# A hybrid trunk on one core: 50 units of the second layer's MLP weights get their lower parts beside the first MLP, and the first layer's MLPs end by halves of tokens

## The chip, the cores and the metric

The kernel runs on one core of a Trainium2 chip. The time is the device time of one execution in microseconds (us). The median of the runs counts; one further execution was profiled. The core has five engines that each work through a list of their own in order: TensorE (PE) multiplies matrices into PSUM, VectorE (DVE), ScalarE (ACT) and GpSimd (POOL) work element by element, and SyncE (SP) issues most of the DMAs. An instruction that waits holds up everything behind it in its engine's list.

## The reference

A decoder trunk of two layers for 1024 tokens of width 1024. Layer 0 mixes the tokens with a state-space model (S5), layer 1 with an attention in which an indexer picks 256 keys for each query. A squared-ReLU MLP of width 4096 follows each mixer. Every sub-layer has a norm before and one after it. All is in float32.

```python
def sq_relu_mlp(h, w1, w2):
    a = jax.nn.relu(h @ w1)
    return (a * a) @ w2

def reference(...):
    h = x
    for i in range(DEPTH):
        pre = rms_norm(h, norm_g[i, 0])
        mix = s5_mixer(pre, ...) if i % 2 == 0 else dsa_mixer(pre, ...)
        h = h + rms_norm(mix, norm_g[i, 1])
        ff = sq_relu_mlp(rms_norm(h, norm_g[i, 2]), mlp_w1[i], mlp_w2[i])
        h = h + rms_norm(ff, norm_g[i, 3])
    return h
```

## The kernel before

**Precision.** A product of float32 matrices is made of three matmuls of a shorter type. Each operand is split into an upper part (a rounded copy) and a lower part (what the rounding left). `mm3` (lines 156 to 161) then adds upper by upper, upper by lower and lower by upper.

**A weight unit.** The weights come in units of 128 x 1024 numbers, 512 KB. `unit` (line 119) loads one into a buffer `wr` (three of them) from SP's queue (line 127). In two halves of 512 columns ACT makes the upper part (line 142) and a subtraction the lower part (line 143), on DVE for the first half and on POOL for the second. Both land in a buffer `wh` of 2 x 512 numbers (six of them, so three units). A unit feeds 24 matmuls of 512 columns.

**The halves of the sequence.** All of the work is done for 512 tokens at a time; the first 512 tokens are half 0, the others half 1. A block is 128 x 2 x 512 numbers: 256 of the 1024 features for 512 tokens, and four blocks are one activation.

**An MLP.** `mlp` (line 281) does one layer's MLP for one half. It has 32 units of w1 and 32 of w2. `pair` (line 297) computes two units of w1, applies ReLU (line 306), squares (line 308) and splits. For each of eight chunks `c` four units of w2 add to four accumulators `acc` in SBUF (line 341). A generator `side` may be handed over. After every unit `beside` (line 289) draws steps from it, `per` of them, after `wait` units without any; these steps are written down with a priority of 500 over the MLP's own. With `finish` (line 316), which the last MLP of the kernel uses, the last four units are loaded into buffers of their own (`wl`, eight). Then the last chunk is done for 256 tokens and again for the other 256 (`th`), and `finish` is called after each with its part of the accumulators.

**The norms.** `post_norm` (line 221) takes an MLP's or a mixer's result, sums its squares (`squares`, line 179: squares on ACT, sums of blocks at line 193, then small matmuls with ones at line 196), takes the inverse root (`rsqrt`, line 163), spreads it over the partitions by PE transposes (line 238) and a copy (line 240), multiplies (line 252) and adds the residual (line 262), which comes back from DRAM (`hd`). `pre_norm` (line 199) multiplies by the gain and splits into upper and lower parts (lines 208 and 209), then sums squares again. `att_r` (line 1165) turns the inverse root into tables for the rotary embedding, with PE transposes (line 1179) of what ACT copies (line 1177).

**The order of the work.** In `run` (line 1242): S5 for both halves; the MLP of layer 0, half 0, without side work (line 1257), called the first MLP here; its norms (line 1258); the MLP of layer 0, half 1 (line 1267), the second MLP, and beside it half 0's projections and attention; its norms (line 1269); half 0's attention output and the index projections of half 1 (lines 1271 to 1275); the residual of half 0 (line 1287); the MLP of layer 1, half 0 (line 1289), the third MLP, and beside it half 1's projections, top-k and attention; at last the MLP of layer 1, half 1 (line 1298), the fourth, with `finish`.

**Who sets each engine's order.** The kernel writes the operations down in program order. A planner then simulates them with modelled costs, takes at each moment the ready operation of the highest priority, fixes every engine's list and every buffer's address from that, and adds the semaphores. The chip keeps to those lists even where its times differ from the modelled ones. The names of the buffers in the profile are those of the pools' tags and tiles; MLP activations appear as `b`, PSUM for the MLP as `m`, for norms as `c`, for the rest as `p`.

Of the kernel before, what the change touches and what calls it, by code (L numbers as in the profile page):

```python
# [7 lines left out]
F32 = mybir.dt.float32  # L8
F32R = mybir.dt.float32r
# [3 lines left out]
ALU = mybir.AluOpType  # L13
AX = mybir.AxisListType

BUFS = {"par": 1, "bc": 2, "tb": 1, "sb": 1, "bb": 2,
        "s5": 14, "cs": 2, "sq5": 8, "cst": 2, "u": 1,
        "x": 8, "xa": 8, "acc": 4, "hid": 9, "b": 22, "ld": 3, "q": 2}
EPS = 1e-6
# [7 lines left out]
STEPS_BEST = 2  # L27

WAIT_OUT = 1

PRIORITY = 500

# [22 lines left out]
class Trunk:  # L55
# [60 lines left out]
        t = t.rearrange("p (a b) -> p a b", a=shape[1]) if len(shape) > 2 else t  # L116
        return t if dt == F32 else t.bitcast(dt)

    def unit(self, src, last=False, heads=False, raw=None):

        nc = self.nc
        self.n += 1
        if raw is None:
            raw = self.wp.tile([128, 1024], F32, name=f"wr{self.n}", tag="wr", bufs=3)
        nc.sync.dma_start(raw, src)
        out = []
        for h in range(2):
            t = self.wp.tile([128, 2, 512], F32R, name=f"wh{self.n}_{h}", tag="wl" if last else "wh",  # L130
                             bufs=8 if last else 6)
            hi, lo = t[:, 0], t[:, 1]
            r = raw[:, h * 512:(h + 1) * 512]
            out.append((hi, lo))
            if heads:
                rs = r.rearrange("p (k h e d) -> p e k h d", h=2, e=2, d=32)
                his, los = [q.rearrange("p (k e h d) -> p e k h d", h=2, e=2, d=32) for q in (hi, lo)]
                parts = [(his[:, e], los[:, e], rs[:, e]) for e in range(2)]
            else:
                parts = [(hi, lo, r)]  # L140
            for ph, pl, pr in parts:
                nc.scalar.activation(ph, pr, AF.Copy)  # L142
                (nc.gpsimd if h else nc.vector).tensor_sub(pl, pr, ph.bitcast(F32))  # L143
        return out
# [51 lines left out]
            nc.tensor.matmul(ps[:, j:j + 1], acc[:, j * 128:(j + 1) * 128], self.ones, start=True, stop=True)  # L196
        return ps[:, :n // 128]

    def pre_norm(self, h, gi, tag="b", square=True):


        nc = self.nc
        out = []
        for j, b in enumerate(h):
            hi, lo = [self.blk([128, 2, 512], F32R, tag=tag) for _ in range(2)]
            for q in range(2):
                g = self.gain[:, gi, 2 * j + q:2 * j + q + 1]
                nc.scalar.activation(hi[:, q], b[:, q], AF.Copy, scale=g)
                nc.vector.scalar_tensor_tensor(lo[:, q], b[:, q], g, hi.bitcast(F32)[:, q],  # L209
                                               op0=ALU.mult, op1=ALU.subtract)  # L210
            out.append((hi, lo))
        s = self.squares(h, nc.gpsimd.tensor_add if square else nc.vector.tensor_add)
        r = self.small([128, 4], F32, "kept")
        nc.vector.tensor_scalar(r, s, 1.0 / 1024, EPS, op0=ALU.mult, op1=ALU.add)
        if square:
            nc.vector.scalar_tensor_tensor(r, r, 1024 * EPS, r, op0=ALU.mult, op1=ALU.mult)
        else:
            nc.vector.tensor_copy(r, self.rsqrt(r, 4)[:, :4])
        return out, r

    def post_norm(self, f, gi, h, e=None, reorder=False, last=None, aside=False):
# [56 lines left out]
            self.nc.sync.dma_start(dst[j], h[j])  # L278


    def mlp(self, L, x, side=None, per=0, wait=0, finish=None):


        nc = self.nc
# [4 lines left out]
        def beside():  # L289
            due[0] += self.per  # L290
            self.units += 1
            while side and due[0] >= 1:
                due[0] -= 1
                with self.tc.high_priority(offset=PRIORITY):
                    next(side, None)

        def pair(p):
            r = self.blk([128, 2, 512], tag="hid")
            for j in range(2):
                w = self.unit(w1[L, 2 * p + j])  # L300
                ps = self.pm()
                for kt in range(8):
                    o = (kt % 4) * 128
                    self.mm3(ps, [t[:, o:o + 128] for t in w[kt // 4]],
                             [t[:, kt % 2] for t in x[kt // 2]], kt == 0, kt == 7)
                nc.scalar.activation(r[:, j], ps, AF.Relu)  # L306
                if j:
                    nc.scalar.activation(r, r, AF.Square)  # L308
                    hid.append(self.split(r, [128, 2, 512], hi_dve=True, tag="hid"))
                beside()  # L310

        acc = []
        for c in range(8):
            while len(hid) < min(2 * c + 3 + (c >= 6), 16):
                pair(len(hid))
            if finish and c == 7:
                ws = [self.unit(w2[L, c, d], last=True) for d in range(4)]
                for th in range(2):
                    n = slice(256 * th, 256 * th + 256)
                    for d, w in enumerate(ws):  # L320
                        for j in range(2):
                            ps = self.pm()[:, :256]
                            for kt in range(4):
                                self.mm3(ps, [t[:, kt * 128:(kt + 1) * 128] for t in w[j]],
                                         [t[:, kt % 2, n] for t in hid[2 * c + kt // 2]], kt == 0, kt == 3)
                            nc.vector.tensor_add(acc[d][:, j, n], acc[d][:, j, n], ps)
                    finish(n, [t[:, :, n] for t in acc])
                break
            for d in range(4):
                w = self.unit(w2[L, c, d])  # L330
                if c == 0:
                    acc.append(self.blk([128, 2, 512], name="acc", tag="acc"))
                for j in range(2):
                    ps = self.pm()
                    for kt in range(4):
                        self.mm3(ps, [t[:, kt * 128:(kt + 1) * 128] for t in w[j]],
                                 [t[:, kt % 2] for t in hid[2 * c + kt // 2]], kt == 0, kt == 3)
                    if c == 0:
                        nc.scalar.activation(acc[d][:, j], ps, AF.Copy)
                    else:  # L340
                        nc.vector.tensor_add(acc[d][:, j], acc[d][:, j], ps)  # L341
                beside()
        for _ in side or ():
            pass
# [897 lines left out]
    def run(self, out):  # L1242
# [8 lines left out]
        def residual(hf, f, gi, src, dst, r2=None):  # L1251
            h = self.post_norm(f, gi, self.load_h(src[hf]), r2)
            self.store_h(dst[hf], h)
            return h

        self.nc.sync.dma_start(self.rope, a["rope"])
        acc = self.mlp(0, xn[0][0])
        x1, r = self.pre_norm(residual(0, acc, 3, hd[0], hd[1], xn[0][1]), 4, square=False)
        self.att_r(0, r)
        self.att_start()  # L1260

# [2 lines left out]
            yield from self.projections(0, x1)  # L1264
            yield from self.attention_a()

        acc = self.mlp(0, xn[1][0], first(), PER_A, WAIT_A)
        xo = finished(self.att_in(0, "x"))
        x1, r = self.pre_norm(residual(1, acc, 3, hd[0], hd[1], xn[1][1]), 4, square=False)
        self.att_r(1, r)  # L1270
        for _ in self.att_out(xo, "hid"):
            pass
# [13 lines left out]
        self.scratch_tag = "acc"  # L1286
        xn[0] = self.pre_norm(residual(0, fA, 5, hd[1], hd[2]), 6, tag="x")
        self.scratch_tag = "b"
        acc = self.mlp(1, xn[0][0], second(), PER_B[0])
        self.store_h(out[0], self.post_norm(acc, 7, self.load_h(hd[2][0]), xn[0][1]))  # L1290
        h = [t() for t in self.load_h(hd[2][1], "x")]
        x, e = xn[1]
# [93 lines left out]
```

## Time and profile before

| | |
|---|---|
| median of 3 runs | 2271.27 us (2270.7 to 2272.05) |
| the profiled execution | 2264.73 us |
| its span, first to last instruction | 2262.6 us |
| granted TensorE clock, mean | 0.978 |
| matmul instructions | 10376 |
| read from HBM, written to it | 229.02 MB, 34.67 MB |

The profile is one execution. Its windows view gives, for each stretch of the span, how long each engine was busy and with how many instructions, the granted clock of PE as a share, the mean busy share of the 16 DMA engines and the GB/s they moved. The lines view groups instructions by line, engine and shapes: busy time, the mean duration in ns, the idle time before them and what ended it. The waits view gives for an engine's line what it waited for: us in total, times, longest. A matmul's end is modelled and successive matmuls overlap, so a stretch without idle time shows PE as fully busy.

### The profile page before, as it was taken

Reading aid. Unit: us, or ns where it says so; the run is one execution under the profiler, and the core shown is the slowest. Engines: PE = TensorE matmul, PEld = TensorE weight load, DVE = VectorE, ACT = ScalarE, POOL = GpSimd, SP = SyncE. Lnnn points to the kernel's source line nnn. Section 1 sums busy time; section 2 is a strip of 40 time slices with the busy share of each in tenths; the row PEclk is TensorE's granted clock in tenths of the full one; section 3 lists DMA queues with packets and bytes.
Section 4 is the critical chain, followed back from the end, with each engine's and each line's share of the span. In section 5 each row is a group of like instructions: output and inputs, shape, how many; then the busy total and the mean of one; then the engine's idle time right before and its main releaser. Section 6 shows DMA issues by size and latency. Waiting matters only on the chain.

```text
span 2262.6 us, 29481 instructions
## 1 busy us (share of the span) xinstructions
PE 2153.9 (95%) x10376; PEld 1778.6 (79%) x10376; DVE 1428.8 (63%) x2756; ACT 1083.2 (48%) x2024; POOL 706.5 (31%) x593
## 2 busy tenths in 40 slices
PE   8998999999989999999988988999999899999997
PEld 4677788888878888888867866888788687888886
DVE  8667943333745687555686889998767477333335
ACT  5436633333543575555463555787456353333332
POOL 1114632222346423222347533222311135222222
PEclk9999999999999999999999999999999999999998
DMA  7113432333437653445446533334222434423231
GB/s 292 30 32 124 160 111 96 100 94 102 131 105 208 154 132 107 117 107 163 143 146 174 163 102 103 96 82 101 79 81 74 144 137 154 147 84 111 85 112 38
DMA packets 115892, 266.81 MB, mean 118 GB/s; under 512 B 14240, under 2 KB 49568, under 8 KB 115744
## 3 DMA queue, kind: packets, MB, share of 16 engines
q1 hardware_dynamic: 101840, 240.77, 33.3%
q0 software_dynamic: 12672, 23.07, 5.4%
q8 instruction: 82, 1.34, 0.3%
q10 hardware_dynamic: 1232, 1.08, 0.1%
q14 instruction: 66, 0.54, 0.1%
HBM read 229.02 MB, written 34.67 MB: 117 GB/s over the span
## 4 chain that ended last, share of the span: by engine, by line
PE 73%; DVE 14%; ACT 5%; issue 5%; POOL 1%; DMA 1%; SPq 0%; DVEq 0%; ACTq 0%; POOLq 0%
PE m L159 17%; PE m L160 17%; PE m L161 17%; PE m L636 2%; PE p L159 2%; PE p L161 2%; PE p L160 2%; PE p L1082 2%; PE p L1062 2%; DVE wh L143 1%; DVE b L252 1%; PE p L1091 1%; PE p L1090 1%; DVE b L209 1%; ACT junk L1000 1%
## 5 line engine op out<-in xcount | busy, mean ns | idle before, releaser
L159 PE MATMUL m<-b,wh 128*128 128x512 f32 (+1 forms) x2208 | 859.9, 392 | 25.0 <-DVE acc L341 11.0
L160 PE MATMUL m<-b,wh 128*128 128x512 f32 (+1 forms) x2208 | 856.6, 390 | 5.1 <-DVE b L209 4.7
L161 PE MATMUL m<-b,wh 128*128 128x512 f32 (+1 forms) x2208 | 855.0, 390 | 4.3 <-DVE wh L143 4.3
L143 POOL TENSOR_TENSOR wh<-wr,wh 128x512 fp32r<-128x512 f32 (+1 forms) x342 | 440.8, 1294 | 1223.7 <-ACT wh L142 1139.8
L142 ACT ACTIVATE wh<-wr 128x512 fp32r<-128x512 f32 (+1 forms) x684 | 395.3, 592 | 502.7 <-PE m L161 416.2
L159 PEld LDWEIGHTS m<-b,wh 128*128 128x128 f32 x2208 | 418.4, 190 | 113.1 <-DVE acc L341 11.6
L161 PEld LDWEIGHTS m<-b,wh 128*128 128x128 f32 x2208 | 418.5, 190 | 89.3 <-DVE wh L143 5.1
L160 PEld LDWEIGHTS m<-b,wh 128*128 128x128 f32 x2208 | 418.8, 190 | 88.3 <-DVE b L209 6.0
L143 DVE TENSOR_TENSOR wh<-wr,wh 128x512 fp32r<-128x512 f32 (+1 forms) x342 | 266.6, 787 | 294.3 <-ACT wh L142 284.1
L341 DVE TENSOR_TENSOR acc<-acc,m 128x512 f32<-128x512 f32 x216 | 147.1, 682 | 154.0 <-PE m L161 152.3
L306 ACT ACTIVATE b<-m 128x512 f32<-128x512 f32 x128 | 76.2, 595 | 163.6 <-PE m L161 160.6
L150 DVE CAST b<-b 128x1024 fp32r<-128x1024 f32 x68 | 58.1, 854 | 126.8 <-ACT b L308 120.5
L161 PE MATMUL p<-b,wh 128*128 128x512 f32 (+1 forms) x304 | 114.6, 387 | 6.7 <-DVE wh L143 6.7
L159 PE MATMUL p<-b,wh 128*128 128x512 f32 (+1 forms) x304 | 112.9, 388 | 3.2 <-ACT b L747 3.2
L160 PE MATMUL p<-b,wh 128*128 128x512 f32 (+1 forms) x304 | 115.9, 386 | 0.0
L1086 ACT ACTIVATE pt<-p 128x512 fp32r<-128x512 f32 (+1 forms) x160 | 83.6, 553 | 65.6 <-PE p L1082 63.2
L1087 DVE TENSOR_TENSOR pt<-p,pt 128x512 fp32r<-128x512 f32 (+1 forms) x160 | 99.0, 630 | 24.5 <-ACT pt L1086 24.3
L1069 ACT ACTIVATE s<-s,ring 128x128 f32<-128x128 f32 (+7 forms) x128 | 98.5, 772 | 31.7 <-DVE ring L1066 31.3
L1000 ACT ACTIVATE junk<-b,ring 128x512 bf16<-128x512 f32 (+2 forms) x90 | 80.6, 896 | 58.4 <-DVE ring L996 51.8
L1062 PE MATMUL p<-kt,q 128*128 128x512 f32 (+2 forms) x384 | 98.5, 363 | 0.0
L1082 PE MATMUL p<-con,s 128*128 128x128 f32 x576 | 93.8, 272 | 0.8 <-DVE ring L1066 0.7
L1066 DVE CUSTOM_DVE_ANT_0 s<-p,nb 128x512 f32<-128x512 f32 (+3 forms) x128 | 72.6, 583 | 32.8 <-PE p L1062 26.7
(314 smaller groups left out, 2738.8 us busy)
## 6 DMA issues: line engine op xcount, KB each, us to landing
wr<-in_w_dram SPq DMA_DIRECT2D x256, 512.0 KB, 3.7
wr<-in_wa_dram SPq DMA_DIRECT2D x32, 512.0 KB, 3.7
q<-qd POOLq DMA_DIRECT2D x64, 256.0 KB, 5.5
ld<-hd SPq DMA_DIRECT2D x24, 512.0 KB, 6.1
hd<-b SPq DMA_DIRECT2D x16, 512.0 KB, 4.6
qd<-b SPq DMA_DIRECT2D x128, 64.0 KB, 2.0
wr<-in_wao_dram SPq DMA_DIRECT2D x16, 512.0 KB, 3.7
q<-qi POOLq DMA_DIRECT2D x24, 256.0 KB, 4.6
```

Of the source, the lines that this page charges most:

```text
L142: nc.scalar.activation(ph, pr, AF.Copy)
L143: (nc.gpsimd if h else nc.vector).tensor_sub(pl, pr, ph.bitcast(F32))
L159: mm(ps, w[0], x[0], start=start, stop=False)
L160: mm(ps, w[0], x[1], start=False, stop=False)
L161: return mm(ps, w[1], x[0], start=False, stop=stop)
L341: nc.vector.tensor_add(acc[d][:, j], acc[d][:, j], ps)
L1000: nc.scalar.activation(junk[:, 1, :W[j]], keys[j].bitcast(F32), AF.Sign, bias=neg[:, j:j + 1], accum_out=cnt[:, j:j + 1])
L1062: nc.tensor.matmul(ps[:, :m], qt[:, v, 2 * hp + k, :], self.K[c][g // 2][:, g % 2, :m], start=v == 0, stop=v == 1)
L1069: nc.scalar.activation(s, s, AF.Exp, bias=least, scale=-1.0, accum_out=self.sums[:, h:h + 1])
L1082: nc.tensor.transpose(pt[:, kk, k, :], P[k][:, (k0 + kk) * 128:(k0 + kk + 1) * 128], self.ident)
L1086: nc.scalar.activation(ph[:, :nk], pt[:, :nk], AF.Copy)
L1087: nc.vector.tensor_sub(pl[:, :nk], pt[:, :nk], ph.bitcast(F32)[:, :nk])
```

## The change

1. **Lower parts in DRAM.** A new generator, `lower_parts`, loads each of the first 50 of layer 1's 64 MLP units into a buffer of a new tag `pr` (nine buffers, three for a unit), makes the upper part on ACT and the lower part on DVE, 1024 columns at a time, and stores the lower part to a DRAM tile. Before each load ACT copies one element of the newest result of the MLP (`pace`) into the load's buffer, so that the load comes after it. The generator is the side work of the first MLP, one unit for each weight unit after the first eight, without raised priority.
2. **Their use.** In the third MLP `unit` makes only the upper part of those 50 units, on ACT, and loads the lower part from DRAM by two DMAs of 256 KB from SP. The fourth MLP is unchanged.
3. **Ends by halves.** The first and second MLP get a `finish`: after each 256 tokens of the last chunk their post-norm, the store of the residual and the pre-norm's upper and lower parts and inverse root for those 256 tokens. In the second MLP the load of attention's output (`att_in`) is written down at the first of these calls.

```diff
-BUFS = {"par": 1, "bc": 2, "tb": 1, "sb": 1, "bb": 2,
+BUFS = {"par": 1, "pr": 9, "bc": 2, "tb": 1, "sb": 1, "bb": 2,
...
+LOWER = 50
...
-    def unit(self, src, last=False, heads=False, raw=None):
+    def unit(self, src, last=False, heads=False, raw=None, lo=None):
...
+            if lo is not None:
+                nc.scalar.activation(hi, r, AF.Copy)
+                nc.sync.dma_start(low.bitcast(F32), lo[:, h * 512:(h + 1) * 512])
+                continue
...
-    def pre_norm(self, h, gi, tag="b", square=True):
+    def pre_norm(self, h, gi, tag="b", square=True, into=None):
...
-            hi, lo = [self.blk([128, 2, 512], F32R, tag=tag) for _ in range(2)]
+            hi, lo = into[0][j] if into else [self.blk([128, 2, 512], F32R, tag=tag) for _ in range(2)]
...
-        r = self.small([128, 4], F32, "kept")
+        r = into[1] if into else self.small([128, 4], F32, "kept")
...
+    def units_of(self, L):
+
+        w1, w2 = self.a["w1"], self.a["w2"]
+        done = 0
+        for c in range(8):
+            n = max(done, min(2 * c + 3 + (c >= 6), 16))
+            for k in range(2 * done, 2 * n):
+                yield ("w1", k), w1[L, k]
+            done = n
+            for d in range(4):
+                yield ("w2", c, d), w2[L, c, d]
+
+    def lower_parts(self, L):
+
+        nc = self.nc
+        dst = self.dp.tile([LOWER, 128, 1024], F32, name="lower")
+        self.lower = {}
+        for k, (key, src) in zip(range(LOWER), self.units_of(L)):
+            raw = self.blk([128, 1024], name="raw", tag="pr")
+
+            nc.scalar.activation(raw[:, 0:1], self.pace[:, 0:1], AF.Copy)
+            nc.sync.dma_start(raw, src)
+            hi, lo = [self.blk([128, 1024], F32R, tag="pr") for _ in range(2)]
+            nc.scalar.activation(hi, raw, AF.Copy)
+            nc.vector.tensor_sub(lo, raw, hi.bitcast(F32))
+            nc.sync.dma_start(dst[k], lo.bitcast(F32))
+            self.lower[key] = dst[k]
+            yield
+
+    def mlp(self, L, x, side=None, per=0, wait=0, finish=None, lower={}, first=True):
...
-                with self.tc.high_priority(offset=PRIORITY):
+                with self.tc.high_priority(offset=PRIORITY if first else 0):
                     next(side, None)
...
-                w = self.unit(w1[L, 2 * p + j])
+                w = self.unit(w1[L, 2 * p + j], lo=lower.get(("w1", 2 * p + j)))
...
                 nc.scalar.activation(r[:, j], ps, AF.Relu)
+                self.pace = r[:, j]
...
             if finish and c == 7:
+                for _ in side or ():
+                    pass
...
-                w = self.unit(w2[L, c, d])
+                w = self.unit(w2[L, c, d], lo=lower.get(("w2", c, d)))
...
+                    self.pace = acc[d][:, j]
...
+        def halves(hf, first=lambda: None):
+
+            x = [tuple(self.blk([128, 2, 512], F32R) for _ in range(2)) for _ in range(4)]
+            r = self.small([128, 4], F32, "kept")
+
+            def take(n, f):
+                if not n.start:
+                    first()
+                m = slice(n.start // 128, n.stop // 128)
+
+                def load(j):
+                    t = self.blk([128, 2, 512], name="ld", tag="ld")[:, :, :256]
+                    self.nc.sync.dma_start(t, hd[0][hf][j][:, :, n])
+                    return t
+
+                h = self.post_norm(f, 3, [lambda j=j: load(j) for j in range(4)], xn[hf][1][:, m])
+                for j in range(4):
+                    self.nc.sync.dma_start(hd[1][hf][j][:, :, n], h[j])
+                self.pre_norm(h, 4, square=False, into=([[t[:, :, n] for t in b] for b in x], r[:, m]))
+
+            return take, x, r
+
         self.nc.sync.dma_start(self.rope, a["rope"])
-        acc = self.mlp(0, xn[0][0])
-        x1, r = self.pre_norm(residual(0, acc, 3, hd[0], hd[1], xn[0][1]), 4, square=False)
+        take, x1, r = halves(0)
+        self.mlp(0, xn[0][0], self.lower_parts(1), 1, 8, finish=take, first=False)
...
-        acc = self.mlp(0, xn[1][0], first(), PER_A, WAIT_A)
-        xo = finished(self.att_in(0, "x"))
-        x1, r = self.pre_norm(residual(1, acc, 3, hd[0], hd[1], xn[1][1]), 4, square=False)
+        side = first()
+        xo = []
+        take, xb, r = halves(1, lambda: xo.extend(finished(self.att_in(0, "x"))))
+        self.mlp(0, xn[1][0], side, PER_A, WAIT_A, finish=take)
+        x1 = xb
...
-        acc = self.mlp(1, xn[0][0], second(), PER_B[0])
+        acc = self.mlp(1, xn[0][0], second(), PER_B[0], lower=self.lower)
```

More of the change, by code (lines that the diff above doesn't have):

```diff
@@ L131, in unit @@
                              bufs=8 if last else 6)
-            hi, lo = t[:, 0], t[:, 1]
+            hi, low = t[:, 0], t[:, 1]
             r = raw[:, h * 512:(h + 1) * 512]
-            out.append((hi, lo))
+            out.append((hi, low))
+            if lo is not None:
+                nc.scalar.activation(hi, r, AF.Copy)
+                nc.sync.dma_start(low.bitcast(F32), lo[:, h * 512:(h + 1) * 512])
+                continue
             if heads:
                 rs = r.rearrange("p (k h e d) -> p e k h d", h=2, e=2, d=32)
-                his, los = [q.rearrange("p (k e h d) -> p e k h d", h=2, e=2, d=32) for q in (hi, lo)]
+                his, los = [q.rearrange("p (k e h d) -> p e k h d", h=2, e=2, d=32) for q in (hi, low)]
                 parts = [(his[:, e], los[:, e], rs[:, e]) for e in range(2)]
             else:
-                parts = [(hi, lo, r)]
+                parts = [(hi, low, r)]
             for ph, pl, pr in parts:
@@ L217, in pre_norm @@
         else:
-            nc.vector.tensor_copy(r, self.rsqrt(r, 4)[:, :4])
+            n = r.shape[-1]
+            nc.vector.tensor_copy(r, self.rsqrt(r, n)[:, :n])
         return out, r
@@ L278, in store_h @@
             self.nc.sync.dma_start(dst[j], h[j])
-    def mlp(self, L, x, side=None, per=0, wait=0, finish=None):
+    def units_of(self, L):
[23 more added lines that the diff above has]
+    def mlp(self, L, x, side=None, per=0, wait=0, finish=None, lower={}, first=True):
         nc = self.nc
```

## The prediction

> **What bounds the kernel now.** I read the page's sums first, then the busy times by window (one row for each stage), then the waits of TensorE (PE) in the windows where it idles, and last the durations of the instructions that the change adds or takes away.
>
> ```profile
> span 2262.6 us, 29481 instructions
> PE 2153.9 (95%) x10376; PEld 1778.6 (79%) x10376; DVE 1428.8 (63%) x2756; ACT 1083.2 (48%) x2024; POOL 706.5 (31%) x593
> ```
> ```profile
> core 0: us, PE busy (x) PEld busy (x) DVE busy (x) ACT busy (x) POOL busy (x), PEclk, DMA share, GB/s
> 0.00:50.00 50.00, 43.12 (x114) 20.54 (x115) 47.26 (x223) 25.97 (x42) 7.87 (x12) 1.00 0.85 319
> 350.00:400.00 50.00, 50.00 (x222) 41.39 (x222) 16.59 (x23) 16.99 (x27) 12.16 (x10) 1.00 0.28 95
> 595.00:660.00 65.00, 58.35 (x263) 48.11 (x262) 41.78 (x55) 33.04 (x61) 22.56 (x18) 0.92 0.36 116
> 1105.00:1215.00 110.00, 95.55 (x417) 77.35 (x417) 86.31 (x108) 54.38 (x102) 61.40 (x47) 0.92 0.47 150
> 1240.00:1400.00 160.00, 141.17 (x642) 115.06 (x641) 139.21 (x301) 85.44 (x183) 66.61 (x58) 0.97 0.43 124
> 1400.00:1580.00 180.00, 179.20 (x975) 153.53 (x973) 166.70 (x451) 132.82 (x256) 39.47 (x42) 1.00 0.39 94
> 1580.00:1640.00 60.00, 55.76 (x280) 46.41 (x279) 44.73 (x80) 27.04 (x52) 19.58 (x13) 0.97 0.30 84
> 1640.00:1770.00 130.00, 119.77 (x724) 104.30 (x723) 86.49 (x192) 77.18 (x145) 16.31 (x17) 0.98 0.30 83
> 2222.00:2234.00 12.00, 12.00 (x102) 12.00 (x102) 6.23 (x16) 6.37 (x13) 0.00 (x0) 1.00 0.01 1
> ```
>
> PE is the bound: 95% of the span. The first MLP (row 350 to 400) runs without a gap, 222 matmuls of 512 columns in 50 us, so 0.225 us each and 24 x 0.225 = 5.41 us for one weight unit. Time can only come from where PE idles, and what matters here is idle in four places: 6.65 us after the first MLP (595 to 660), 14.45 us after the second (1105 to 1215), 18.83 us in the early part of the third (1240 to 1400), 4.24 us later in it (1580 to 1640). Between the last two (1400 to 1580) PE is full and so is VectorE (DVE), 166.70 of 180. A long wait costs more than its idle time, since the granted clock is low behind it: 0.92 over 65 us is 5.2 us of clock. I count half of that, as PE mostly stands still meanwhile. So the four places are worth 6.65 + 2.6 = 9.2, 14.45 + 4.4 = 18.9, 18.83 + 2.4 = 21.2 and 4.24 + 0.9 = 5.1 us.
>
> What ended the waits, in 595 to 660 (first two lines), 1105 to 1215 (five) and 1290 to 1400 (three):
> ```profile
> PE c L196 <- DVE b L193: 3.8, 1, 3.8
> PE p L1179 <- ACT b L1177: 1.9, 1, 1.9
> ...
> PE p L161 <- DVE wh L143: 3.9, 1, 3.9
> PE p L1179 <- ACT b L1177: 2.9, 2, 1.4
> PE m L159 <- DVE b L828: 2.8, 1, 2.8
> PE c L238 <- DVE ring L171: 2.1, 1, 2.1
> PE c L196 <- DVE b L193: 2.0, 1, 2.0
> ...
> PE m L159 <- DVE acc L341: 5.4, 4, 2.1
> PE m L159 <- ACT b L306: 2.9, 4, 0.8
> PE p L161 <- DVE wh L143: 2.8, 1, 2.8
> ```
>
> After both MLPs PE stands at the norms' small matmuls (L196, L1179), which come in its list before the next MLP's; DVE is not yet done with the norm. In the third MLP it waits on DVE for weight halves (L143) and for sums that free PSUM (L341): DVE's queue is what is late.
>
> **The change part by part.** First the 50 lower parts made beside the first MLP. Rows of 300 to 590, then DMA issues:
> ```profile
> L308 ACT ACTIVATE b<-b 128x1024 f32<-128x1024 f32 x13 | 13.7, 1052 | 0.0
> L168 ACT ACTIVATE ring<-ring 128x4 f32<-128x4 f32 x1 | 0.2, 205 | 1.2 <-DVE ring L167 1.2
> L153 DVE TENSOR_TENSOR b<-b,b 128x1024 fp32r<-128x1024 f32 x13 | 15.8, 1218 | 0.3
> ```
> ```profile
> wr<-in_w_dram SPq DMA_DIRECT2D x256, 512.0 KB, 3.7
> hd<-b SPq DMA_DIRECT2D x16, 512.0 KB, 4.6
> xt<-in_xt_dram SPq DMA_DIRECT2D x8, 512.0 KB, 9.9
> out_dram<-acc SPq DMA_DIRECT2D x4, 256.0 KB, 2.5
> b<-rd SPq DMA_DIRECT2D x16, 256.0 KB, 6.0
> ```
>
> Each unit adds on ScalarE (ACT) a copy of 1024 (as L308, 1.05) and a one-element pace copy (0.21, as L168), on DVE a subtraction of 1024 (as L153, 1.22), and on SP's queue one load and one store of 512 KB. ACT and DVE are busy 16.99 and 16.59 us in 50 now, with 222 / 24 = 9.25 units, so 1.84 and 1.79 each; they come to 3.1 and 3.0 of 5.41. DMA goes from one transfer of 0.524 MB a unit to three: 291 GB/s. At 319 GB/s for a share of 0.85 that is 0.78 of the DMA engines; at 95 for 0.28 it is 0.86. It fits. PE is full here, so a gain is excluded and the lower bound is 0. Nothing waits behind the pace copy but ACT's own list: the ReLUs (L306) that free PSUM and the weights' upper parts (L142), which PE needs up to two units later, 10.8 us. Upper bound: the slower rival below. I take +2 us.
>
> The two ends by halves. The last four units become 192 matmuls of 256 columns instead of 96 of 512. Row 2222 to 2234 has them: 12.00 / 102 = 0.118 us, so 22.6 against 21.6 us: +1.0 us for each MLP. For that the norm of the first half, and its share of the next pre-norm, run beside 11 us of matmuls, and the chain behind the last matmul is one half as wide. DVE's costliest line of it, 595 to 640, then the same line 256 wide at the kernel's own halved end, 2220 on:
> ```profile
> L252 DVE SCALAR_TENSOR_TENSOR acc<-acc,con,rb 128x512 f32<-128x512 f32 x8 | 8.6, 1137 | 0.0
> ...
> L252 DVE SCALAR_TENSOR_TENSOR acc<-acc,con,rb 128x256 f32<-128x256 f32 x8 | 4.7, 661 | 1.3 <-ACT rb L240 1.3
> ```
>
> Half the width takes 661 / 1137 = 0.58 of the time, so DVE's work rises a little, and what stands behind the last matmul falls to a little over half. The loads and stores of hd double in number, not in bytes. They sit on SP behind the weight loads, which are prefetched, and I cost them at nothing; if that cover goes, each is 256 KB, 2.5 to 6.0 us. I take half of the waits at each end: -4.6 + 1.0 = -3.6 after the first MLP (bounds -8.2 and +1.0), -9.4 + 1.0 = -8.4 after the second (bounds -17.9 and +1.0). What is late next after the second is the following residual's norm, the same DVE list (L171, L828 above), which is why I don't take more.
>
> The third MLP reads 50 lower parts. In 1240 to 1400:
> ```profile
> L143 DVE TENSOR_TENSOR wh<-wr,wh x28: 409/684/1801, 1241.1 to 1399.3; 128x512 fp32r<-128x512 f32 x18, 128x256 fp32r<-128x256 f32 x10
> L127 SPq DMA_DIRECT2D wr<-in_w_dram x17: 328/352/388, 1242.3 to 1392.6; - x17
> ```
> 17 units are loaded here, one in 9.4 us; the third MLP has only begun, so all are among its first 50. DVE loses 17 x 0.684 = 11.6 us of 139.21, POOL as many subtractions. Two more DMAs a unit are issued, at 0.35 us each on SP; 17 x 0.524 MB in 160 us is 56 GB/s, which lifts DMA's share from 0.43 to 0.62. The lower part now waits on SP until its wh buffer is free; behind it stand later weights, qd's stores and od's. The raw load three units on waited for the same buffer already, through the split, so the queue's rhythm stays. From free to ready takes 2.5 to 6.0 us instead of 0.62 + 0.69; PE comes back to that buffer two units later, 18.8 us here. Where DVE's list is what is late, 11.6 us less of it is at most 11.6 us less waiting, but 2.9 of the waits end on ACT: I take -10 (bounds 0 and -21.2). In 1400 to 1580 PE is full: 0. In 1580 to 1640 I take -1.5 of 5.1 (bounds 0 and -5.1). The tail to 1770 is attention's own: 0.
>
> DVE's tiny L1006, 1240 to 1345 and 1345 to 1400:
> ```profile
> L1006 DVE COPY_PREDICATED con<-ring 128x2 int32<-128x2 int32 x18 | 8.2, 455 | 0.6
> L1006 DVE COPY_PREDICATED con<-ring 128x2 int32<-128x2 int32 x13 | 2.1, 163 | 0.6 <-DVE ring L1005 0.2
> ```
> [...]
>
> Sum: +2 - 3.6 - 8.4 - 10 - 1.5 = **-21.5 us**. The profiled execution took 2264.73 us (span 2262.6), so 2243.2 by itself; the median of the runs stands at 2271.27, 6.5 higher, and I forecast that: 2249.8, say **2250 us**.
>
> **The rivals.** *The relief is hidden.* The third MLP may be paced by attention's step-by-step top-k and by PSUM buffers, as the L306 waits suggest; against it, DVE is busy 87%. Without the 11.5 us: 2261.3.
>
> *More is freed.* If DVE's list was all that was late, both places in the third MLP empty, 21.2 + 5.1 in place of 11.5: 2235.
>
> *New waits at the halves.* There are twice as many norm points in PE's list. If they gain nothing and each MLP's gets one more 3.8 us wait, then +2 - 11.5 + 2.0 + 7.6 = 0.1: 2271, no change. Against it, at the kernel's own halved end PE meets the first half's L196 without waiting (first line). The others are the wait of 3.8 us today and what follows it:
> ```profile
> 2235.98 0.50 PE L196 MATMUL c<-con,b 128*128 128x1 f32 x4
> ...
> 630.18 1.84 PE L196 MATMUL c<-con,b 128*128 128x1 f32 x8 [3.82 <-DVE b L193]
> 632.45 0.63 PE L161 MATMUL m<-b,wh 128*128 128x512 f32 x1
> 632.88 0.63 PE L159 MATMUL m<-b,wh 128*128 128x512 f32 x1
> ```
> Matmuls start 0.43 us apart there, not 0.225. [...]
>
> *Slower: the pace copy blocks ACT.* Nine buffers hold three units, so a unit's cycle of load, copy, subtraction and store may take 3 x 5.41 = 16.2 us. With 3.7 and 4.6 for the transfers it takes 10.6; with 9.9 for both, as seen at the 0.85 share, 22.1. From 16.2 on, that is from transfers of 7.0, the pace copy waits for its buffer, and the ReLUs and upper parts wait behind it. At 8.0 each the cycle is 18.3, 0.7 us a unit, 50 units: +35, less the 23.5 gained elsewhere: 2283.
>
> *It does not do what it says.* If the lower parts are planned too late, so that the third MLP's first loads wait for stores, it loses the 11.5 and waits about a load and a store, 3.7 + 4.6, for some three units, 25: 2286.
>
> **How the numbers follow.** Forecast 0.44 (its own range 2240 to 2260), hidden relief 0.16, more freed 0.10, new waits 0.13, blocked ACT 0.13, late parts 0.04. Half of the rivals' prices are guesses at how often, so the range runs from 2230, a little past "more freed", to 2278, short of the two slow ones, which hold the 0.17 left out. A change of 0.2%, 4.5 us, is about what a measurement of this kernel can tell. Faster: 0.44 + 0.16 + 0.10 = 0.70; same 0.13; slower 0.17.
>
> **What would show it.** Right: the first MLP still 222 matmuls in 50 us with DMA's share near 0.8; at its end no L196 wait of 3 us; DVE without L143 on most units of the third MLP and PE idle there under 10 us in the 160. Wrong: ACT idle at the pace line and PE gaps in 300 to 580; waits on the lower part's DMA in the third MLP; PE waits at L196 or L238 inside a halved end.

## The result: slower, and the profile after

The changed kernel took **2299.65 us** (median of four runs, 2297.11 to 2309.14) beside 2271.66 for the kernel before on the same chip: a ratio of 1.0132, 95% interval 1.0109 to 1.0154. (This ratio is that of the means, without the one run of the kernel before that took 2282.1 us, so it is not quite that of the medians.) I had forecast 2250.

First the page's sums of the changed kernel, then its windows. From the end of the first MLP on it runs about 33 us late, so the later windows are set 33 us behind those quoted of before.

```profile
span 2295.3 us, 30616 instructions
PE 2174.3 (95%) x10568; PEld 1798.2 (78%) x10568; DVE 1463.9 (64%) x2858; ACT 1133.9 (49%) x2166; POOL 644.6 (28%) x547
```
```profile
300.00:350.00 50.00, 50.00 (x222) 41.40 (x222) 27.21 (x29) 22.05 (x41) 13.20 (x9) 1.00 0.75 253
400.00:450.00 50.00, 44.77 (x187) 36.15 (x186) 24.74 (x28) 21.37 (x38) 11.79 (x8) 0.93 0.75 252
450.00:500.00 50.00, 45.56 (x189) 36.84 (x188) 25.94 (x30) 21.37 (x38) 11.79 (x8) 0.93 0.79 253
595.00:660.00 65.00, 59.67 (x323) 52.94 (x323) 48.17 (x97) 27.60 (x56) 17.11 (x12) 0.92 0.43 144
1138.00:1248.00 110.00, 94.29 (x414) 76.97 (x414) 86.99 (x140) 55.44 (x116) 54.65 (x42) 0.91 0.47 146
1273.00:1433.00 160.00, 146.84 (x665) 120.66 (x664) 128.87 (x290) 86.44 (x186) 47.70 (x44) 0.96 0.60 178
1433.00:1613.00 180.00, 178.34 (x969) 152.97 (x969) 150.74 (x432) 133.08 (x256) 12.51 (x22) 1.00 0.55 153
1613.00:1673.00 60.00, 58.80 (x304) 49.15 (x303) 37.65 (x74) 28.15 (x53) 6.95 (x6) 1.00 0.50 152
```

Two rows carry the result. From 400 to 450, where PE had been full with 222 matmuls, it does 187. And the third MLP (1273 to 1433) did gain: PE is busy 146.84 us against 141.17, DVE 128.87 against 139.21.

To compare stages of all kernels I use one number worked out from the trace, **PE's lost time**: the distances between the starts of successive matmuls, less what a matmul of that width takes at a granted clock of 1.00 (0.227 us for 512 columns, 0.175 for 384, 0.120 for 256, 0.110 for 128, about the median distances between matmuls of one width in the trace of before; for one or 16 columns, which start 0.03 to 0.11 us apart there, 0.050 is my estimate). A distance counts for the stretch in which the later of its two matmuls starts. The number holds idle time and low clock alike, and no extra work. It comes from one profiled execution of each kernel, so small differences mean little: over the first 280 us, which no edit touches, the kernels of this document lose between 71.4 and 74.3 us.

| PE's lost time, us | 300 to 700: first MLP, its end | 1000 to 1250: second MLP's end | 1250 to 1700: third MLP |
|---|---|---|---|
| before | 12.2 | 24.6 | 37.4 |
| changed (last column 1250 to 1750) | 46.1 (to 750) | 27.5 | 29.0 |

The first MLP and its end lose 33.9 us more, the second end 2.9 more, the third MLP 8.4 less, and 192 extra narrow matmuls cost 2 x 1.0. That is 30.4 of the 32.7 us between the spans.

What PE waited for from 350 to 600, and ScalarE's list around 390 us:

```profile
PE m L165 <- DVE b L156: 10.4, 4, 4.3
PE m L166 <- DVE b L159: 4.4, 4, 1.2
PE m L167 <- POOL wh L149: 2.0, 3, 1.0
```
```profile
385.65 1.06 ACT L311 ACTIVATE b<-raw 128x1024 fp32r<-128x1024 f32 x1 [3.94 <-DMA raw<-in_w_dram]
386.62 0.18 ACT L308 ACTIVATE raw<-acc 128x1 f32<-128x1 f32 x1
386.71 1.14 ACT L148 ACTIVATE wh<-wr 128x512 fp32r<-128x512 f32 x2
391.39 1.06 ACT L311 ACTIVATE b<-raw 128x1024 fp32r<-128x1024 f32 x1 [3.54 <-DMA raw<-in_w_dram]
392.35 0.18 ACT L308 ACTIVATE raw<-acc 128x1 f32<-128x1 f32 x1
392.44 0.62 ACT L148 ACTIVATE wh<-wr 128x512 fp32r<-128x512 f32 x1
392.97 0.58 ACT L343 ACTIVATE b<-m 128x512 f32<-128x512 f32 x1
393.44 0.62 ACT L148 ACTIVATE wh<-wr 128x512 fp32r<-128x512 f32 x1
397.55 1.06 ACT L311 ACTIVATE b<-raw 128x1024 fp32r<-128x1024 f32 x1 [3.49 <-DMA raw<-in_w_dram]
```

(L308 is the pace copy, L311 the copy of 1024, L148 the weights' upper parts, L156 and L159 the hidden activation's split, L343 the ReLU.) PE waits on VectorE, and VectorE's list hangs on ScalarE's: from 300 to 550 its subtraction of 1024 finds the engine idle for 117.8 us, nearly all of it until ScalarE's copy of the same unit.

```profile
L312 DVE TENSOR_TENSOR b<-raw,b 128x1024 fp32r<-128x1024 f32 x41 | 50.2, 1225 | 117.8 <-ACT b L311 111.3 <-ACT raw L308 6.5
```

Read ScalarE's list as a loop. The pace copy of a unit at 392.35 releases that unit's load, which SP issues at 392.56. The copy of the same unit waits for the load to land and starts at 397.55. The **next** pace copy stands behind that copy, so only one load is ever in flight (none of the 50 is issued before the one ahead of it has landed), and a round takes 6.16 us (391.39 to 397.55), where PE needs 5.41 for a unit. The DMA issues say how long a load takes to land (last column, median us, over the whole execution):

```profile
wr<-in_w_dram SPq DMA_DIRECT2D x256, 512.0 KB, 4.0
raw<-in_w_dram SPq DMA_DIRECT2D x50, 512.0 KB, 4.5
lower<-b SPq DMA_DIRECT2D x50, 512.0 KB, 4.9
wh<-lower SPq DMA_DIRECT2D x100, 256.0 KB, 3.3
```

That was my **theory** for the experiments: 50 rounds, each about 0.7 us too long, are 35 us. The rivals: three times the traffic slows the weights' loads; the added copies and subtractions themselves are too much for ScalarE and VectorE; the halved ends cost it.

### The profile page after: what moved, and what is told of

Same layout as the page of the kernel before. It is cut to its first block, busy times and chain, and to the rows that moved or that the text cites. A ratio compares the mean times of both kernels' runs of the same rounds, so it can differ in the third digit from the quotient of the medians.

```text
span 2295.3 us, 30616 instructions
## 1 busy us (share of the span) xinstructions
PE 2174.3 (95%) x10568; PEld 1798.2 (78%) x10568; DVE 1463.9 (64%) x2858; ACT 1133.9 (49%) x2166; POOL 644.6 (28%) x547
## 4 chain that ended last, share of the span: by engine, by line
PE 52%; DVE 10%; issue 5%; ACT 5%; DMA 3%; POOL 1%; SPq 0%; ACTq 0%; DVEq 0%; POOLq 0%
PE m L165 13%; PE m L167 13%; PE m L166 13%; PE p L1103 2%; PE p L1123 2%; PE p L167 2%; PE p L165 2%; PE p L166 2%; DMA raw<-in_w_dram 2%; PE p L1131 1%; DVE wh L149 1%; PE p L1132 1%; PE p L970 1%; ACT junk L1041 1%; DVE junk L1003 1%
## 5 line engine op out<-in xcount | busy, mean ns | idle before, releaser
L165 PE MATMUL m<-b,wh 128*128 128x512 f32 (+1 forms) x2272 | 875.3, 387 | 30.8 <-DVE b L156 10.4
L166 PE MATMUL m<-b,wh 128*128 128x512 f32 (+1 forms) x2272 | 872.3, 386 | 8.8 <-DVE b L159 4.4
L167 PE MATMUL m<-b,wh 128*128 128x512 f32 (+1 forms) x2272 | 871.4, 386 | 7.9 <-DVE wh L149 4.8
L149 POOL TENSOR_TENSOR wh<-wr,wh 128x512 fp32r<-128x512 f32 (+1 forms) x292 | 378.6, 1303 | 1026.0 <-ACT wh L148 974.9
L165 PEld LDWEIGHTS m<-b,wh 128*128 128x128 f32 x2272 | 434.3, 191 | 117.8 <-DVE b L156 12.1
L167 PEld LDWEIGHTS m<-b,wh 128*128 128x128 f32 x2272 | 433.9, 191 | 92.3 <-DVE wh L149 6.3
L166 PEld LDWEIGHTS m<-b,wh 128*128 128x128 f32 x2272 | 434.0, 191 | 91.5 <-DVE b L159 6.0
L148 ACT ACTIVATE wh<-wr 128x512 fp32r<-128x512 f32 (+1 forms) x584 | 328.8, 583 | 298.2 <-PE m L167 202.3
L149 DVE TENSOR_TENSOR wh<-wr,wh 128x512 fp32r<-128x512 f32 (+1 forms) x292 | 244.1, 844 | 222.3 <-ACT wh L148 212.9
L381 DVE TENSOR_TENSOR acc<-acc,m 128x512 f32<-128x512 f32 x200 | 135.6, 680 | 80.4 <-PE m L167 79.5
L312 DVE TENSOR_TENSOR b<-raw,b 128x1024 fp32r<-128x1024 f32 x50 | 61.3, 1225 | 140.1 <-ACT b L311 133.5
L311 ACT ACTIVATE b<-raw 128x1024 fp32r<-128x1024 f32 x50 | 53.0, 1060 | 172.5 <-DMA raw<-in_w_dram 156.3
L343 ACT ACTIVATE b<-m 128x512 f32<-128x512 f32 x128 | 75.7, 591 | 122.3 <-PE m L167 117.7
L167 PE MATMUL p<-b,wh 128*128 128x512 f32 (+1 forms) x304 | 116.0, 391 | 6.7 <-DVE wh L149 6.7
L165 PE MATMUL p<-b,wh 128*128 128x512 f32 (+1 forms) x304 | 115.8, 398 | 6.1 <-ACT b L788 3.2
L156 DVE CAST b<-b 128x1024 fp32r<-128x1024 f32 x68 | 59.7, 877 | 91.1 <-ACT b L346 86.8
L166 PE MATMUL p<-b,wh 128*128 128x512 f32 (+1 forms) x304 | 117.4, 390 | 0.0
```

The costliest lines, as they stand in the source:

```text
L165: mm(ps, w[0], x[0], start=start, stop=False)
L166: mm(ps, w[0], x[1], start=False, stop=False)
L167: return mm(ps, w[1], x[0], start=False, stop=stop)
```

## The experiments

Each was timed beside the kernel before on the same chip; ratios are to it, with their 95% interval.

**Lower parts without halved ends.** Both first-layer MLPs end as before:

```diff
-        take, x1, r = halves(0)
-        self.mlp(0, xn[0][0], self.lower_parts(1), 1, 8, finish=take, first=False)
+        acc = self.mlp(0, xn[0][0], self.lower_parts(1), 1, 8, first=False)
+        x1, r = self.pre_norm(residual(0, acc, 3, hd[0], hd[1], xn[0][1]), 4, square=False)
```
(and the second MLP likewise)

> The lower parts are made and used, but both first-layer MLPs end as before. Theory (one load in flight: ScalarE's copy of a unit waits for the load that its own pace copy released, and the next pace copy stands behind it, 6.1 us a unit against 5.41 of matmuls): the first MLP still loses about 33 us, the third still gains 6 to 8, so 2292 to 2298, close to the changed kernel. Rival (the halved ends are what costs, and the first MLP's lost time comes with them): 2262 to 2266, with 222 matmuls per 50 us in the first MLP.

Measured: 2289.7 us, ratio 1.0091 (1.0073 to 1.0109). The first MLP still loses: 191 matmuls from 400 to 450. So most of the loss is there without the halved ends, in the making of the lower parts. The time lies just under the expected range, and 0.41% (9 us) under the changed kernel's, which was not in my theory: the halved ends cost something there. In the two traces 5.1 us of it stand behind the second MLP.

**Halved ends without lower parts.** The first MLP gets no side work, the third makes its own:

```diff
-        self.mlp(0, xn[0][0], self.lower_parts(1), 1, 8, finish=take, first=False)
+        self.mlp(0, xn[0][0], finish=take)
...
-        acc = self.mlp(1, xn[0][0], second(), PER_B[0], lower=self.lower)
+        acc = self.mlp(1, xn[0][0], second(), PER_B[0])
```

> No lower parts are made or used; both first-layer MLPs end by halves. Theory (the loss sits in the making of the lower parts): the first MLP is full again, the two halved ends are worth 0 to +6 us together, so 2270 to 2278. Rival (the halved ends are what costs): about 2300. My forecast's step for the halves, -12 us, would give 2260.

Measured: 2270.67 us, ratio 1.0003 (0.9989 to 1.0018): no change, not the 12 us that I had forecast.

**Load a step ahead.** The same bytes, copies, subtractions and stores in another order, and one more one-element copy a unit: the next unit's pace copy and load stand ahead of this unit's copy.

```diff
+            if unit:
+                raw = self.blk([128, 1024], name="raw", tag="pr")
                 nc.scalar.activation(raw[:, 0:1], self.pace[:, 0:1], AF.Copy)
-            nc.sync.dma_start(raw, src)
+                nc.sync.dma_start(raw, unit[1])
+            if behind:
+                key, b = behind
                 hi, lo = [self.blk([128, 1024], F32R, tag="pr") for _ in range(2)]
-            nc.scalar.activation(hi, raw, AF.Copy)
+                nc.scalar.activation(hi.bitcast(F32)[:, 0:1], self.pace[:, 0:1], AF.Copy)
+                nc.scalar.activation(hi, b, AF.Copy)
...
+            behind = (unit[0], raw) if unit else None
```

> The whole change, but the load of the next unit is issued before the copy of this unit, so two loads are in flight; same bytes, same copies, subtractions and stores, and one more one-element copy a unit. Theory (one load in flight): ScalarE's idle at the copy of 1024 falls from 172 us to under 60, the first MLP is back at about 222 matmuls per 50 us, and the time falls by 25 to 33 us to 2266 to 2275. Rival (three times the traffic slows the weights' loads): stays at 2297 to 2302, as the bytes per unit are the same. Rival (the added work on ScalarE and VectorE itself): stays at 2297 to 2302 too.

Measured: 2262.66 us, ratio 0.9975 (0.9962 to 0.9988), 36 us under the changed kernel by the ratios, a little more than the 25 to 33 expected. The order of TensorE's instructions is the same in both traces from the first to the last, and behind the first MLP so is that of VectorE, ScalarE and GpSimd: the planner changed nothing else in them. ScalarE's copy of 1024 from 300 to 550 (busy us, mean ns, idle before it), first of the changed kernel, then with the load ahead:

```profile
L311 ACT ACTIVATE b<-raw 128x1024 fp32r<-128x1024 f32 x40 | 42.4, 1061 | 142.7 <-DMA raw<-in_w_dram 129.9 <-issue 12.8
L343 ACT ACTIVATE b<-m 128x512 f32<-128x512 f32 x20 | 11.6, 580 | 0.0
...
L308 ACT ACTIVATE raw<-b 128x1 f32<-128x1 f32 x21 | 3.9, 187 | 0.0
```
```profile
L317 ACT ACTIVATE b<-raw 128x1024 fp32r<-128x1024 f32 x45 | 47.8, 1061 | 5.9 <-DMA raw<-in_w_dram 4.6
L350 ACT ACTIVATE b<-m 128x512 f32<-128x512 f32 x25 | 15.0, 599 | 47.6 <-PE m L167 41.2 <-DVE b L318 4.3 <-DMA wr<-in_w_dram 2.1
```

40 units in 250 us against 45; ScalarE's wait for the load falls from 142.7 us to 5.9, and what it waits for now is PE (L350 <-PE m L167 41.2). Two windows of the same kernel:

```profile
400.00:450.00 50.00, 50.00 (x222) 41.46 (x221) 28.82 (x34) 28.04 (x55) 12.98 (x10) 1.00 0.85 289
450.00:500.00 50.00, 50.00 (x222) 41.42 (x222) 27.26 (x33) 27.62 (x53) 11.80 (x9) 1.00 0.86 287
```

PE is full again although the DMA engines are busier than in the changed kernel (0.85 against 0.75) and so are ScalarE and VectorE. The weights' loads do land later there, in 5.2 us in the median from 300 to 550 against 3.5 in the kernel before (first line of the kernel before, second with the load ahead), but they are issued early enough that PE does not wait for them. Traffic and added work fall as causes.

```profile
wr<-in_w_dram SPq DMA_DIRECT2D x46, 512.0 KB, 3.5
wr<-in_w_dram SPq DMA_DIRECT2D x46, 512.0 KB, 5.2
```

**No wait for the load at all.** Copy and subtraction read a constant block that stays in SBUF; the stored lower parts are those of the constant. The block takes a tenth buffer of `pr` and is written once, at the start; the order of TensorE's instructions is again the same.

```diff
-            nc.scalar.activation(hi, raw, AF.Copy)
-            nc.vector.tensor_sub(lo, raw, hi.bitcast(F32))
+            nc.scalar.activation(hi, own, AF.Copy)
+            nc.vector.tensor_sub(lo, own, hi.bitcast(F32))
```

> The whole change with the same pace copies, loads, copies, subtractions and stores, but the copy and the subtraction read a constant block that stays in SBUF, so ScalarE never waits for a load to land. The stored lower parts are those of the constant, not of the weights. Theory (the wait for the load's landing): the first MLP is back at 222 matmuls per 50 us, 2263 to 2271, about 33 us under the changed kernel. Rivals (traffic; added work on ScalarE and VectorE): stays at 2297 to 2302, since traffic and work are unchanged.

Measured: 2258.56 us, ratio 0.9958 (0.9941 to 0.9976), under the expected 2263 to 2271 but on the theory's side. From 300 to 350 PE is full at a DMA share of 0.88:

```profile
300.00:350.00 50.00, 50.00 (x222) 41.43 (x221) 27.84 (x32) 26.70 (x45) 11.81 (x9) 1.00 0.88 303
```

The loss of the first MLP is settled. What remained were the ends and the third MLP, and I took the load ahead as the base.

**Ahead, without halved ends** (the edit of the first experiment on top):

> Loads a step ahead, as in the run with the load ahead, but both first-layer MLPs end as before. Theory (in the traces the halved first end gains about 5 us and the halved second end loses about 5, so the two cancel): 2258 to 2266, level with the run with the load ahead (2263). Rival (the halves cost 10 us, as between the changed kernel and the run with the lower parts only): 2250 to 2255.

Measured: 2259.01 us, ratio 0.9953 (0.9939 to 0.9967). Within the theory's range in microseconds, but by the ratios 5 us under the run with the halves, where the theory had them level; the intervals just overlap.

**Ahead, first end by halves** (only the second MLP ends as before):

> Loads a step ahead, the first MLP ends by halves, the second as before. Theory (the first halved end is worth -5 us, the second +5): 2254 to 2260, about 5 us under both the run with the load ahead and the one without halves. Rival (my forecast: the second halved end is worth more than the first): 2266 to 2272, as -8.4 us is lost. Rival (neither end matters): 2260 to 2265.

Measured: 2262.01 us, ratio 0.9961 (0.9949 to 0.9973). A miss: no gain over the run without halves. The time is in the range of the rival by which neither end matters (2260 to 2265).

**Ahead, lower parts made and not used** (the third MLP without `lower=self.lower`):

> Loads a step ahead, both ends by halves, the lower parts are made and stored, but the third MLP makes its own again as before. It prices their use alone. Theory (PE's excess in the third MLP differs by 3 to 5 us between the traces): 2265 to 2270. My forecast (11.5 us in the third MLP): 2272 to 2277. Rival (their use gains nothing): 2260 to 2265.

Measured: 2272.25 us, ratio 1.0008 (0.9998 to 1.0018). By the ratios the use of the lower parts is worth 0.33%, 7.5 us, with about 3.7 to either side; the expected microseconds had assumed a kernel before of 2268, and it took 2271 here. That lies between the theory's 3 to 5 us and my forecast's 11.5.

**A second copy in place of eight subtractions.** In the norm of the attention's residual behind the second MLP, ScalarE writes a second copy where VectorE made the lower parts, so these are not the reference's.

```diff
+        none = tag == "x" and gi == 6
...
+                if none:
+                    nc.scalar.activation(lo[:, q], b[:, q], AF.Copy, scale=g)
+                    continue
                 nc.vector.scalar_tensor_tensor(lo[:, q], b[:, q], g, hi.bitcast(F32)[:, q],
```

> The run with the load ahead, but in the norm of the attention's residual of half 0 (the one behind the second halved end) VectorE's eight subtractions for the lower parts are left out; ScalarE writes a second copy in their place, so those lower parts are not the reference's. Theory (behind the halved end PE waits on VectorE's list, in which eight of these of 1.2 to 1.8 us stand ahead of the weight's subtraction): PE's wait of 7.5 us for the weight half near 1190 us falls under 2 us and the time by 4 to 8 us, to 2255 to 2259. Rival (the wait comes from the weight's load or ScalarE's part): the wait stays over 6 us and the time at 2261 to 2265.

Measured: 2253.19 us, ratio 0.9934 (0.9911 to 0.9957). By the ratios that is 9 us under the run with the load ahead, with about 6 to either side, where 4 to 8 were expected. PE's waits from 1100 to 1250, first of the run with the load ahead, then of this one:

```profile
PE p L167 <- DVE wh L149: 7.5, 1, 7.5
PE p L1227 <- ACT b L1225: 5.3, 2, 4.1
PE c L245 <- DVE ring L177: 2.1, 1, 2.1
```
```profile
PE p L1231 <- ACT b L1229: 5.3, 2, 4.1
PE c L249 <- DVE ring L177: 2.1, 1, 2.1
PE p L981 <- DMA q<-qi: 1.8, 1, 1.8
```

The wait of 7.5 us is gone. VectorE's list in the run with the load ahead shows why:

```profile
1180.63 5.78 DVE L215 SCALAR_TENSOR_TENSOR b<-b,con,b 128x512 fp32r<-128x512 f32 x4
...
1188.45 6.93 DVE L215 SCALAR_TENSOR_TENSOR b<-b,con,b 128x512 fp32r<-128x512 f32 x4
...
1197.41 1.83 DVE L149 TENSOR_TENSOR wh<-wr,wh 128x256 fp32r<-128x256 f32 x2
```

PE stands from 1191.8 to 1199.3 for the weight half that L149 makes at 1197.41, behind the second four of the eight subtractions of the next norm.

**Four of the eight on GpSimd**, on the base without halves; what is computed stays the same:

```diff
+                if tag == "x" and gi == 6 and q:
+                    t = self.blk([128, 512])
+                    nc.scalar.activation(t, b[:, q], AF.Copy, scale=g)
+                    nc.gpsimd.tensor_sub(lo[:, q], t, hi.bitcast(F32)[:, q])
+                    continue
```

> Loads a step ahead and both first-layer ends as before, and in the norm of the attention's residual of half 0 four of VectorE's eight subtractions for the lower parts go another way with the same result: ScalarE writes the scaled value to a block of its own and GpSimd subtracts. Theory (behind the second MLP PE waits on VectorE's list): PE's wait for the weight half of 4.3 us near 1195 us falls under 2 us and the time is 2 to 4 us under the run with the load ahead and no halves, 2255 to 2258 where that run is 2259. Rival (GpSimd's work slows VectorE's as much as it relieves it): within 1 us of that run, or over it.

Measured: 2262.92 us, ratio 0.9962 (0.9946 to 0.9978). The wait for the weight half fell from 4.3 to 1.5 us as the theory said, and the time did not fall with it: the theory's range is missed, the rival's number (within 1 us of the run without halves, or over it) is met. The rival's reason is not seen: from 1170 to 1205 VectorE is busy 5.3 us with the four subtractions that are left, against 9.9 with eight.

PE's lost time by stage shows where such gains went (lines as in the first table):

| PE's lost time, us | 300 to 700 | 1000 to 1250 | 1250 to 1700 | ratio |
|---|---|---|---|---|
| before | 12.2 | 24.6 | 37.4 | 1 |
| halves only | 5.6 | 29.0 | 37.8 | 1.0003 |
| ahead (both halves) | 4.5 | 33.2 | 31.5 | 0.9975 |
| no wait | 4.0 | 31.4 | 29.4 | 0.9958 |
| ahead, no halves | 12.7 | 29.2 | 26.0 | 0.9953 |
| ahead, first half | 4.5 | 27.9 | 34.1 | 0.9961 |
| ahead, not used | 4.5 | 30.5 | 37.5 | 1.0008 |
| ahead, second copy | 4.5 | 21.4 | 33.8 | 0.9934 |
| ahead, four on GpSimd | 12.8 | 24.1 | 32.4 | 0.9962 |

The last row loses 5.1 us less behind the second MLP than the run without halves and 6.4 more in the third MLP. How much such a number moves by itself can be read off three kernels whose engines have the same lists from the end of the first MLP on, the changed one, ahead and no wait: 27.5, 33.2 and 31.4 behind the second MLP, 29.0, 31.5 and 29.4 in the third (the changed kernel's stretches hold the same stages, some 33 us late).

## Why the prediction was wrong

**The step that failed is the first term, +2 us.** It said: "Nothing waits behind the pace copy but ACT's own list", and priced what waits for the pace copy. It did not price what ScalarE itself waits for: the copy of 1024 a few instructions on needs the load that the pace copy has just released. In an engine that works in order, that wait holds the ReLUs, the upper parts and the next pace copy: from 300 to 550 ScalarE idles 142.7 us before that copy and 0.0 before these. All its pieces stood in the rows I had quoted: 1.05 for the copy, 0.21 for the pace copy, 0.35 for SP's issue and 3.7 for a load of 512 KB, the weights' of before, make 5.3 us, which leaves 0.1 of the 5.41 of a unit; with 4.6, as a store of 512 KB took, it is 6.2. Measured: 6.16, with loads that land in 4.5. I added busy times (3.1 of 5.41) where a loop with a latency in it sets the rate. In the time this term is 36 us by the reversed order and 40 by the constant block, each with about 6 to either side, where I had +2; in the first stage of the profiled executions it is 41.6 (46.1 against 4.5).

**The slower rival** had the engine, the size (+35) and a wrong wait. Its condition, transfers from 7.0 us on, was not met (4.5 and 4.9), and the pace copies waited 0.0 us for their buffer; the wait stood at the copy of 1024. That the size agrees is luck: it came from transfers of 8.0 us, which were not there.

**First halved end, -3.6: right in its stage, and better.** The pair halves only and before differ by 6.6 there, the pair ahead, first half and no halves by 8.2, less 1.0 for narrow matmuls. With the load ahead PE no longer waits at the small matmuls (L202, the L196 of before) after this MLP. In the time it is not to be found: 0.9961 against 0.9953, with 8.1 us lost again in the third MLP.

**Second halved end, -8.4: no gain, more likely a loss.** Three pairs point that way: halves only against before +4.4, both halves against the first alone +5.3 with the load ahead, and the changed kernel against the run with lower parts and without halves +5.1 (27.5 against 22.4), and 1.0 for narrow matmuls each time. As three kernels with the same lists differ by 5.7 in this stage, the size of the loss is not settled. What the pairs do show is that the 9.4 us of waits that I had counted on were not won. I had named the list that is late next, the following residual's norm on VectorE, and still took half of the waits. That list holds more: with its eight subtractions gone the stage loses 21.4, against 33.2, 31.4 and 27.5 in the three kernels with both halves and the same lists; 2.3 of the 11.8 between it and the run with the load ahead come back in the third MLP. Halves only against before, the halves took away PE's waits at L196 (2.0) and for L828 (2.8), and those for the rotary tables (2.9 to 5.3) and the weight half (3.9 to 8.7) grew by 7.2.

**Third MLP, -10 and -1.5: right in kind, somewhat too large.** 7.5 us in the time, by the run that makes them and does not use them. In the stage 6.0 between that run and its base, 11.4 between before and the run without halves. VectorE's relief came as forecast. From 1240 to 1400, ahead without halves:

```profile
1240.00:1400.00 160.00, 147.78 (x673) 120.09 (x672) 129.12 (x288) 90.12 (x193) 48.81 (x49) 0.97 0.62 181
1580.00:1640.00 60.00, 58.80 (x308) 49.27 (x307) 37.45 (x73) 27.78 (x54) 6.96 (x6) 1.00 0.51 156
```

VectorE has 10.1 us less (139.21 before; I said 11.6), PE 6.6 more, and 3.0 more from 1580 to 1640; the DMA share is the 0.62 forecast. VectorE's two-element copies (L1006 of before, L1054 in the run without halves) hardly got shorter: from 1240 to 1345 they take 435 ns on average, against 455. Those averages mislead, as shortest, median and longest show (the average of the run without halves, then the three numbers of before and of that run):

```profile
L1054 DVE COPY_PREDICATED con<-ring 128x2 int32<-128x2 int32 x17 | 7.4, 435 | 0.7 <-DVE ring L1053 0.2
...
L1006 DVE COPY_PREDICATED con<-ring x18: 163/164/1277, 1280.4 to 1344.0; 128x2 int32<-128x2 int32 x18
L1054 DVE COPY_PREDICATED con<-ring x17: 150/165/1227, 1286.4 to 1341.7; 128x2 int32<-128x2 int32 x17
```

In the kernel before 6 of these 18 copies take 658 to 1277 ns, and just these 6 start while a GpSimd instruction runs; the other 12 take 163 to 166, and each of the 6 ends about 20 ns after that instruction. In the changed kernel, from 1273 to 1378, it is 4 of 17, at 1215 to 1258, and 163 to 166 for the other 13. Beside four of the six it was a weight subtraction; beside all 4 of the changed kernel it is GpSimd's work for the rotary embedding (L870, L873). So the long copies did not end with the weight subtractions that left GpSimd.

**Open.** The third MLP's own code is the same in six of these runs, and it loses 26.0 to 34.1 us. Its waits differ: from 1250 to 1500 with the first end halved PE waits 2.9 us on a DMA that is not among the waits of the run without halves.

```profile
PE p L1110 <- DMA q<-qd: 2.9, 1, 2.9
PE m L165 <- DVE acc L388: 2.7, 1, 2.7
```

Both fall between 1380 and 1410, where PE is busy 23.80 us of 30 at a clock of 0.94; the run without halves is full at 1.00 from 1390 to 1415.

The traces show that the order of all four engines' instructions in this stage differs between these two runs, while in the changed kernel, ahead and no wait it is the same; those three lose 29.0 to 31.5 there. So the planner's new lists may be why a gain of 5 to 8 us ahead of this stage comes back in it. It was not tested with the lists held fixed.

Of the kernels that leave nothing out, the fastest is the one with the load ahead and no halved ends, 0.47% under before (0.33 to 0.61). The intervals of the other three that use the lower parts with the load ahead overlap its own, so their order is not settled.

## What to carry to other kernels

When side work is put on an engine that works in order, look for the loop through it: where an instruction waited for a load that the same engine had released shortly before, the loop's latency, 6.16 us a round, and not ScalarE's busy time, 21.37 of 50 us, set the rate here, against 5.41 for the step of the bound engine. Release the next load before waiting for this one: that took 36 us off here, by the ratios. Shortening one chain gained nothing here (ratio 1.0003 for the halved ends alone), where another list ended last behind the second MLP; take the second list's work away in a trial before paying for the first. And compare the lists of two kernels before reading a small gain: where the edit changed only the stretch that was meant, as with the load ahead, the time can be put down to it.

## What was not expected of the hardware

Three times the weight traffic did not slow PE: at DMA shares of 0.82 to 0.88 the first MLP stays full, although the weights' loads land in 5.2 us there in the median with the load ahead, 3.5 before. And one stall costs more than its length. Behind the wait of 4.29 us in the changed kernel the next matmuls start 1.74 and 0.59 us apart, where just before it they are 0.23 apart; the first of these distances holds a second wait, and the granted clock is 0.50 from 406.4 to 412.0, 0.88 from there to 414 and 1.00 from 414 to 418:

```profile
401.73 0.39 PE L167 MATMUL m<-b,wh 128*128 128x512 f32 x1
406.40 0.79 PE L165 MATMUL m<-b,wh 128*128 128x512 f32 x1 [4.29 <-DVE b L156]
408.14 0.79 PE L166 MATMUL m<-b,wh 128*128 128x512 f32 x1 [0.94 <-DVE b L159]
408.73 0.63 PE L167 MATMUL m<-b,wh 128*128 128x512 f32 x1
```

VectorE's subtraction of 512 columns (L215, L209 of before) took 1264 ns on average in the kernel before, from 1170 to 1205 (743 at its shortest), and 1646 with the load ahead (1223 at its shortest). GpSimd's sums and weight subtractions run beside it in both; what made it longer was not tested.
